# The chunk scan's factors and products kept in a PSUM bank instead of SBUF

## The chip, the cores and the metric

The kernel runs on one core of one Trainium2 chip. A core has five engines that run side by side, each with its own instruction queue in a fixed order: TensorE (PE in the profile, with its weight loads as PEld), VectorE (DVE), ScalarE (ACT), GpSimd (POOL) and SyncE (SP), which issues the DMA transfers. The metric is device time in microseconds, lower is better; a run's time is compared as the median of several executions.

## The reference, cut to what matters

Two layers of a trunk with parallel token mixers are run over 128 context tokens and 512 noisy tokens, width 1024. In each layer the modulated input goes through one wide projection, whose parts feed attention, a state-space branch, a Fourier branch and three gates. The branch that matters here is the state space:

```python
for di in range(2):                               # forward, backward
    bu = einsum(u, bb)                            # complex, per group of 16 channels
    h[t] = lb * h[t - 1] + bu[t]                  # complex, 32 groups x 64 states
    y = y + Re(c * h)
ssm_y = gelu(y)
ssm_y = ssm_y * sigmoid(ssm_y @ w_glu + b_glu)
merged = g_a * (attn @ w_a) + g_s * (ssm_y @ w_s) + g_f * (four @ w_f)
```

The six modulation vectors of a layer are `silu(c) @ w_ada[l] + b_ada[l]`, for two conditioning vectors.

## The kernel before

Activations are stored channels on partitions, tokens along the row, in two halves of 256 and 384 tokens. Every large product is made from operands split into a high and a low fp32r part, so it is three matmuls (lines 129 to 131). A weight tile arrives by DMA (`wraw`, three buffers), ScalarE rounds it to the high part (`wh`, line 111), and VectorE, or GpSimd for the units named in `PZ`, `PU`, `PB` and `PO`, subtracts to get the low part (`wl`, line 112). These splits stand between TensorE and its next weight tile.

**The scan.** The recurrence runs over chunks of 8 tokens: 64 chunks of the noisy tokens, 16 of the context tokens. `ssm_scan` first fills `V` (tile `Vst`, in SBUF) with the chunk inputs: TensorE's products `psv` lie in PSUM banks of the pool tag `ss`, which has two, and are copied out by ScalarE and VectorE (lines 648 to 651). Then come 64 steps on VectorE. A step reads the state row `V[:, s]`, multiplies it by the 8-step transition factors (line 658: 128 x 128 elements, real and imaginary state each against a pair of factors), and adds the two products to row `s + 1` (line 661: two additions). The first 16 steps carry both token groups: two multiplications of 128 x 128 and two additions of 128 x 128; the other 48 steps have one multiplication of 128 x 128 and two additions of 128 x 64. That is 80 multiplications and 128 additions in a layer. The factors are a slice of `L8`, a small SBUF table of both layers; the products lie in `sc`, an SBUF tile with two buffers.

`ssm_out` reads the states (`Hr`, lines 675 to 678), TensorE forms the outputs `psy` in the same two `ss` banks (lines 689 and 691), and VectorE and ScalarE apply the gelu (lines 694 to 698). Its result goes through DRAM to the product with `w_glu`.

**What runs beside it.** The scan is traced inside the stream of the wide projection (`mm_wz`): after its first four tiles the stream goes on with the gates, and the splits of their weights share VectorE's queue with the scan. In layer 0 two more things do. The modulation vectors that layer 0 still needs are made by VectorE as sums along rows of the transposed weights (`ada_rows`, line 276: a `scalar_tensor_tensor` of two SBUF tiles with its elementwise result in the PSUM tile `adjunk`), one step of four such sums each time the stream calls `fill`. And GpSimd makes the state-space tables of layer 1 (`ssm_prep`, lines 576 to 630: products of SBUF tiles, with transposes on TensorE between them), along with the low parts of some weight tiles. In layer 1 there are no such sums and no tables to make, so the same scan has only weight splits beside it.

**Order.** The order within each engine's queue is not written out by hand: the kernel is built with `schedule_with_timeline_sim=True`, by which the builder places instructions on a simulated timeline. A different instruction form can thus move its neighbours in the queues.

Of the kernel before, what the change touches and what calls it, by code (L numbers as in the profile page):

```python
# [10 lines left out]
F32 = mybir.dt.float32  # L11
# [6 lines left out]
DRAM = bass.MemoryType.DRAM  # L18

P = 128  # L20
# [41 lines left out]
class Trunk:  # L62
# [12 lines left out]

    # ---------------------------------------------------------------- helpers
    def mmbank(self, nm):
# [6 lines left out]
    def mmextra(self, n):  # L84
        """n more banks for the main products until the returned stack closes."""
        st = ExitStack()
        self.mmpool = st.enter_context(self.tc.tile_pool(name=f"mmx{self.mmi}", bufs=1, space=PSUM))
        self.mmx = n

        def off():  # L90
            self.mmx = 0
        st.callback(off)
        return st

    def behind(self, ins):
        """What is traced within on the engine of ins is queued behind it."""
        return nullcontext() if ins is None else self.tc.issue_after(ins.ins)

    def ld(self, dst, src):
        """A transfer; the first ones are issued as traced, and all others after them."""  # L100
        i = self.nc.sync.dma_start(dst, src)
        if self.head is not None:
            self.tc.add_manual_dep(i.ins, self.head.name, mybir.DependencyInfo(
                mybir.DependencyClass.NoSync, mybir.DependencyReason.DATA), reason="after the first loads")
        if self.pin:
            self.head = i.ins
        return i
# [25 lines left out]
    def wextra(self, pool, nm, n):  # L133
        """n more units for the weights of a stream."""
        return [[pool.tile([P, 1024], F32R, name=f"{nm}{k}{x}") for x in "hl"] for k in range(n)]

    def stream(self, tiles, operand, consume, lag, extra=(), fill_from=0, loaded=None, order=(1, 0), pool=(), pre=()):
        """tiles: list of (key, unit source, n, offsets); one half `lag` tiles behind the other;
        low parts of the units named in pool are taken by the Pool engine; pre: banks of tiles whose first half is there."""
        loaded = {} if loaded is None else loaded  # L140
        n = len(tiles)

        def go(j, half):
            key, src, width, offs = tiles[j]
            if half == order[0] and j in pre:
                return consume(key, half, pre[j][:, :HW[half]])
            if src not in loaded:
                k = len(loaded) % (4 + len(extra))
                loaded[src] = self.wunit(self.usrc(src), width, extra[k - 4] if k >= 4 else None,
                                         self.nc.gpsimd if len(loaded) in pool else None)  # L150
            h, l = loaded[src]
            pairs = []
            for kt, o in enumerate(offs):
                xh, xl = operand(half, kt, key)
                pairs.append((h[:, o:o + P], l[:, o:o + P], xh, xl))
            ps = self.mmbank(src[0])
            self.mm3(ps[:, :HW[half]], pairs)
            consume(key, half, ps[:, :HW[half]])

        for j in range(n + lag):  # L160
            if j < n:
                go(j, order[0])
            if j >= fill_from:
                self.fill()
            if j >= lag:
                go(j - lag, order[1])
# [8 lines left out]
    def rsqrt(self, out, v, tmp, iters=3):  # L175
        """out = v ** -0.5, v > 0; tmp: two scratch APs of the same shape."""
        nc = self.nc
        a, b = tmp
        nc.vector.tensor_scalar(a.bitcast(I32), v.bitcast(I32), 1, None, op0=OP.logical_shift_right)
        nc.vector.tensor_scalar(out.bitcast(I32), a.bitcast(I32), -1.0, float(0x5F3759DF), op0=OP.mult, op1=OP.add)  # L180
        nc.vector.tensor_scalar(a, v, -0.5, None, op0=OP.mult)
        for _ in range(iters):
            nc.vector.tensor_tensor(b, out, out, OP.mult)
            nc.vector.tensor_tensor(b, b, a, OP.mult)
            nc.vector.scalar_tensor_tensor(out, b, 1.5, out, OP.add, OP.mult)

    # ---------------------------------------------------------------- constants
    def constants(self):
# [6 lines left out]

    # ---------------------------------------------------------------- modulation
    def silu_c(self):
# [17 lines left out]
    def crows(self):  # L215
        """Silu of the conditioning vectors, as rows in DRAM scratch."""
        nc = self.nc
# [10 lines left out]
    def ada_first(self, pool, block):  # L228
        """Shift and scale of the first layer, by channel tiles."""
        nc = self.nc  # L230
# [29 lines left out]
    def ada_rows(self, l, vecs, cuts, part, bufs):  # L260
        """Modulation vectors of a layer as sums along rows of the transposed weights, in steps."""
        nc = self.nc
# [23 lines left out]
    def adpool(self, l):  # L286
        """Modulation vectors of a layer, in idle slots until closed."""
        st = ExitStack()
# [20 lines left out]
    def derive_u(self, l):  # L309
        """Per-channel scale and bias of u from x (first layer) or from the normalised rows."""  # L310
        nc, s, m = self.nc, self.small, self.mod[l]
# [27 lines left out]
    def modsplit(self, src, half, sc, sh, dt, uh, ul):  # L339
        """uh + ul = src * sc + sh on one channel tile of a half."""  # L340
        nc = self.nc
# [15 lines left out]

    # ---------------------------------------------------------------- layer norm
    def shift(self, r, out):
        """Take each token's mean over the channels off, which the layer norm ignores."""  # L360
        nc = self.nc
# [13 lines left out]
    def ln_add(self, st, half, r, dt):  # L375
        """Sums over the channel tiles of r and of its square."""
        nc = self.nc
# [15 lines left out]
    def ln_half(self, st, n, mm=False, later=None):  # L393
        """Banks with rstd and mean * rstd of each token, the same on every partition; mm: banks of the main products."""
        nc, m = self.nc, self.main
# [17 lines left out]
        out = []  # L413
# [6 lines left out]

    # ---------------------------------------------------------------- state-space tables
    def ssm_scalars(self, p, loads):
        """Powers of the discretised transition and of the input factor, both layers."""
        nc, tc = self.nc, self.tc
# [115 lines left out]
    def ssm_open(self):  # L540
        """Pools of the per-layer tables and the loads they start from."""
        st = self.prep = ExitStack()
# [16 lines left out]
    def ssm_prep(self, l, order):  # L559
        """Per-layer stationary operands of the chunked scan, left in DRAM scratch."""  # L560
        nc, tc = self.nc, self.tc
# [70 lines left out]

    # ---------------------------------------------------------------- state-space branch
    def ssm_scan(self, l, z, zp, V, U):
# [3 lines left out]
        for ch in range(8):  # L638
            w = z.tile([P, 4, 2, P], F32, name="wbs", tag="wbs", bufs=2)
            self.ld(w.rearrange("p g r q -> p (g r q)"), self.wbd[l][ch])  # L640
            for hh in range(2):
# [9 lines left out]
                nc.scalar.copy(V[bw, VP + 1:VP + 17, gr], v[bw, :16][:, ::-1])  # L651
        la = self.L8[:, :, 32 * l:32 * l + 32]
        for s in range(64):
            n = 2 if s < 16 else 1
            t = z.tile([P, 2, 2, 64], F32, name="sc", tag="sc", bufs=2)
            for k in range(n):
# [45 lines left out]

    # ---------------------------------------------------------------- one layer
    def layer(self, l):
# [204 lines left out]
    def ln_last(self, s, r, half, g, b, out):  # L909
        """The layer norm that ends the last layer."""  # L910
        nc = self.nc
# [38 lines left out]

    # ---------------------------------------------------------------- Fourier branch
    def fourier(self, fd, fh, fl):
# [53 lines left out]

    # ---------------------------------------------------------------- attention branch
    def qkv(self, l, z):
# [129 lines left out]
    def prompt_heads(self, z, zp, kv, QT, KTt, vt, ah, al):  # L1138
        """The context tokens' attention, four heads of one key head at a time."""
        nc = self.nc  # L1140
# [43 lines left out]

    # ---------------------------------------------------------------- gated MLP
    def ffn(self, l, u2, rh, resid, g2):
# [84 lines left out]

    # ---------------------------------------------------------------- program
    def run(self, layers=NL):
# [70 lines left out]
def _layout(a):  # L1344
    """Host side: slices, transposes, repeats and shape-only constants."""
    f = np.float32
# [101 lines left out]
```

## Time and profile before

| | |
|---|---|
| median of 3 executions | 2339.52 us (2337.55 to 2341.88) |
| profiled execution: span from first to last instruction | 2343.4 us |
| profiled execution: own time | no figure beside the span |
| PE busy | 2201.9 us (94%) |
| VectorE busy | 1699.0 us (73%) |
| ScalarE busy | 874.7 us (37%) |
| GpSimd busy | 627.3 us (27%) |

Busy is the time in which an engine had an instruction in work, so an instruction that has started and is held up counts as busy too. The span is 3.9 us above the median of the timed runs (0.17%). In the views "x" is a number of instructions; PEclk is the mean granted clock of TensorE as a share of its upper level, 2.4 GHz.

### The profile page before, as it was taken

How to read it: one execution, taken by the hardware profiler on the slowest of the kernel's cores; microseconds unless marked ns; L12 is line 12 of the kernel's file. 1: busy time of each engine (PE TensorE's matmuls, PEld its weight loads, DVE VectorE, ACT ScalarE, POOL GpSimd, SP SyncE). 2: the span in 40 equal slices, each digit the busy share in tenths (PEclk: the TensorE clock that was granted, in tenths of full speed). 3: DMA queues.
4: the chain of work that ended last, by engine and by line, in shares of the span. 5: the costliest groups of instructions: out<-in, count | busy, mean ns of one | idle time of the engine just before them, and what ended most of it. 6: DMA issues, size and time to landing. Idle time of an engine off the chain costs nothing.

```text
span 2343.4 us, 40415 instructions
## 1 busy us (share of the span) xinstructions
PE 2201.9 (94%) x15368; PEld 2122.0 (91%) x15368; DVE 1699.0 (73%) x3997; ACT 874.7 (37%) x1781; POOL 627.3 (27%) x603
## 2 busy tenths in 40 slices
PE   5998876998999999999998999999899999999997
PEld 4888776998879999999998999999879999999997
DVE  7779998779655888999986167455765876475476
ACT  4333212433643542332344332334463443243242
POOL 3337765003535410100116000001635420000003
PEclk8999897999999999999999999999999999999998
DMA  9976436664214124545535744742304122222221
GB/s 258 220 248 204 150 112 195 220 192 124 59 32 137 64 73 144 158 142 160 170 100 152 161 148 127 180 156 81 100 1 150 55 72 64 82 73 72 82 73 45
DMA packets 185009, 295.00 MB, mean 126 GB/s; under 512 B 48464, under 2 KB 127472, under 8 KB 184816
## 3 DMA queue, kind: packets, MB, share of 16 engines
q1 hardware_dynamic: 184816, 292.43, 42.4%
q8 instruction: 121, 1.98, 0.4%
q14 instruction: 72, 0.59, 0.1%
HBM read 242.62 MB, written 49.75 MB: 125 GB/s over the span
## 4 chain that ended last, share of the span: by engine, by line
PE 67%; DVE 16%; DMA 6%; issue 2%; ACT 1%; SPq 1%; POOL 1%; ACTq 0%; DVEq 0%; POOLq 0%
PE mm_w_up L130 7%; PE mm_w_up L131 7%; PE mm_w_up L129 7%; DVE adjunk L276 5%; PE mm_w_down L129 4%; PE mm_w_down L131 4%; PE mm_w_down L130 4%; PE mm_wz L130 3%; PE mm_wz L131 3%; PE mm_wz L129 3%; PE mm_pv L1129 2%; DMA araw<-in_w_ada_t_dram 2%; DVE Vst L661 2%; PE S L1171 2%; PE pt L1182 2%
## 5 line engine op out<-in xcount | busy, mean ns | idle before, releaser
L111 ACT CAST wh<-wraw 128x1024 fp32r<-128x1024 f32 (+1 forms) x226 | 234.6, 1038 | 430.5 <-PE mm_w_down L130 107.7
L129 PE MATMUL mm_w_up<-uh,wh 128*128 128x256 f32 (+1 forms) x1280 | 392.6, 309 | 2.6 <-DVE acc L1207 1.8
L130 PE MATMUL mm_w_up<-ul,wh 128*128 128x256 f32 (+1 forms) x1280 | 394.8, 309 | 0.0
L131 PE MATMUL mm_w_up<-uh,wl 128*128 128x256 f32 (+1 forms) x1280 | 394.3, 309 | 0.0
L112 POOL TENSOR_TENSOR wl<-wraw,wh 128x1024 fp32r<-128x1024 f32 x64 | 157.1, 2458 | 847.5 <-ACT wh L111 824.1
L276 DVE SCALAR_TENSOR_TENSOR adjunk<-araw,cb 128x512 f32<-128x512 f32 (+2 forms) x384 | 276.1, 719 | 45.7 <-DMA araw<-in_w_ada_t_dram 40.9
L131 PE MATMUL mm_wz<-uh,wl 128*128 128x384 f32 (+1 forms) x832 | 269.0, 324 | 23.2 <-DVE wl L112 23.2
L112 DVE TENSOR_TENSOR wl<-wraw,wh 128x1024 fp32r<-128x1024 f32 (+1 forms) x162 | 205.7, 1270 | 109.6 <-ACT wh L111 108.7
L129 PE MATMUL mm_wz<-uh,wh 128*128 128x384 f32 (+1 forms) x832 | 268.5, 324 | 5.2 <-ACT uh L111 3.5
L1207 DVE SCALAR_TENSOR_TENSOR acc<-mm_w_up,cw,acc 128x127 f32<-128x127 f32 (+2 forms) x616 | 229.3, 400 | 52.1 <-ACT acc L1213 32.9
L130 PE MATMUL mm_wz<-ul,wh 128*128 128x384 f32 (+1 forms) x832 | 267.0, 321 | 0.1
L129 PEld LDWEIGHTS mm_w_up<-uh,wh 128*128 128x128 f32 x1280 | 241.8, 189 | 3.2 <-issue 2.1
L130 PEld LDWEIGHTS mm_w_up<-ul,wh 128*128 128x128 f32 x1280 | 242.4, 189 | 0.5 <-DVE ul L112 0.5
L131 PEld LDWEIGHTS mm_w_up<-uh,wl 128*128 128x128 f32 x1280 | 242.3, 189 | 0.5 <-POOL wl L112 0.4
L131 PE MATMUL mm_w_down<-hh,wl 128*128 128x384 f32 (+1 forms) x656 | 203.0, 311 | 0.0
L130 PE MATMUL mm_w_down<-hh,wh 128*128 128x384 f32 (+1 forms) x656 | 202.8, 310 | 0.0
L129 PE MATMUL mm_w_down<-hh,wh 128*128 128x384 f32 (+1 forms) x656 | 200.7, 311 | 1.9 <-ACT wh L111 1.9
L131 PEld LDWEIGHTS mm_wz<-uh,wl 128*128 128x128 f32 x832 | 165.0, 198 | 25.3 <-DVE wl L112 24.4
L129 PEld LDWEIGHTS mm_wz<-uh,wh 128*128 128x128 f32 x832 | 165.7, 199 | 7.4 <-ACT uh L111 3.8
L130 PEld LDWEIGHTS mm_wz<-ul,wh 128*128 128x128 f32 x832 | 164.8, 198 | 2.3 <-issue 1.4
L129 PEld LDWEIGHTS mm_w_down<-hh,wh 128*128 128x128 f32 x656 | 123.4, 189 | 2.2 <-ACT wh L111 2.2
L1213 ACT ACTIVATE acc<-mm_w_up,cw 128x256 f32<-128x256 f32 (+1 forms) x176 | 107.2, 613 | 46.0 <-PE mm_w_up L131 44.5
(444 smaller groups left out, 5316.9 us busy)
## 6 DMA issues: line engine op xcount, KB each, us to landing
wraw<-in_w_up_dram SPq DMA_DIRECT2D x88, 512.0 KB, 3.6
wraw<-in_wz_dram SPq DMA_DIRECT2D x64, 512.0 KB, 3.9
araw<-in_w_ada_t_dram SPq DMA_DIRECT2D x48, 512.0 KB, 3.8
wraw<-in_w_down_dram SPq DMA_DIRECT2D x32, 512.0 KB, 3.6
araw<-in_w_ada_t_dram SPq DMA_DIRECT2D x32, 384.0 KB, 4.1
wraw<-in_w_br_dram SPq DMA_DIRECT2D x24, 512.0 KB, 3.7
td<-gt SPq DMA_DIRECT2D x48, 192.0 KB, 3.1
tl<-td SPq DMA_DIRECT2D x48, 192.0 KB, 3.1
```

The costliest lines, as they stand in the source:

```text
L111: nc.scalar.copy(h, src)
L112: return (eng or nc.vector).tensor_tensor(l, src, h.bitcast(F32), OP.subtract)
L129: mm(ps, wh, xh, start=j == 0, stop=False)
L130: mm(ps, wh, xl, start=False, stop=False)
L131: mm(ps, wl, xh, start=False, stop=j == n - 1)
L276: nc.vector.scalar_tensor_tensor(junk[:, :k.stop - k.start], raw[:, d], 1.0, cb[v], OP.mult, OP.mult, accum_out=part[:, c, vec - a, dt + d ...
L661: nc.vector.tensor_tensor(o, o, t[:, a, :n], OP.add)
L1129: nc.tensor.matmul(po[64 * hh:64 * hh + 64, :256], vt[:, kt + 1, kv * 64:kv * 64 + 64], PT[hh][:, kt], start=kt == 0, stop=kt == 5, tile_p ...
L1171: nc.tensor.matmul(S[:, b, :384], q, kt[:, hl, P + b * 384:P + (b + 1) * 384], start=hl == 0, stop=hl == 1)
L1182: nc.tensor.transpose(pt[:, j * P:(j + 1) * P], p[:, (3 * b + j) * P:(3 * b + j + 1) * P], self.ident)
L1207: nc.vector.scalar_tensor_tensor(o, src, w, o, OP.mult, OP.add)
L1213: nc.scalar.activation(acc, ps, AF.Identity, bias=b, scale=w1)
```

## The change

The factors of the layer and the products move from SBUF into one PSUM bank. The bank is a third user of the pool tag `ss`: columns 0 to 255 take the products, columns 256 to 383 the factors, which one ScalarE copy in each layer brings there from `L8`. The SBUF tile `sc` with its two buffers is gone, so consecutive steps write their products to the same place. Each multiplication now reads one operand from SBUF (`V`) and one from PSUM and writes to PSUM; each addition reads one operand from SBUF (`V`) and one from PSUM and writes to SBUF. The number, shapes and engine of the scan's instructions stay as they are, as do the modulation sums. The rest of the diff removes comments and docstrings.

```diff
@@ ssm_scan
-        la = self.L8[:, :, 32 * l:32 * l + 32]
+        bank = zp.tile([P, 512], F32, name="scb", tag="ss", bufs=2)
+        la = bank[:, 256:384].rearrange("p (a g r) -> p a g r", a=2, r=2)
+        nc.scalar.copy(la, self.L8[:, :, 32 * l:32 * l + 32])
+        t = bank[:, :256].rearrange("p (a k q) -> p a k q", a=2, k=2)
         for s in range(64):
             n = 2 if s < 16 else 1
-            t = z.tile([P, 2, 2, 64], F32, name="sc", tag="sc", bufs=2)
             for k in range(n):
                 h = V[:, s + VP * k].rearrange("p (g r) -> p r g", r=2).unsqueeze(3).broadcast_to((P, 2, 32, 2))
                 nc.vector.tensor_tensor(t[:, :, k].rearrange("p a (g r) -> p a g r", r=2), h, la, OP.mult)
```

## Rows read from the trace of the kernel before

**Rows 1.** Busy time of the whole page.
```profile
PE 2201.9 (94%) x15368; PEld 2122.0 (91%) x15368; DVE 1699.0 (73%) x3997; ACT 874.7 (37%) x1781; POOL 627.3 (27%) x603
```

**Rows 2.** Busy time by stretch: PE, PEld, DVE, ACT, POOL, PEclk, DMA share, GB/s.
```profile
80.00:207.00 127.00, 118.98 (x983) 114.27 (x982) 98.58 (x188) 48.20 (x121) 65.11 (x80) 0.96 0.87 244
207.00:365.00 158.00, 116.56 (x823) 111.45 (x821) 149.50 (x311) 33.11 (x67) 109.33 (x128) 0.85 0.43 141
207.00:440.00 233.00, 185.94 (x1307) 178.67 (x1306) 207.37 (x428) 55.60 (x112) 142.27 (x158) 0.85 0.53 165
440.00:600.00 160.00, 146.29 (x1017) 141.45 (x1016) 132.15 (x388) 60.70 (x128) 31.50 (x21) 0.98 0.52 160
1369.00:1457.00 88.00, 88.00 (x602) 88.00 (x601) 70.62 (x227) 23.66 (x40) 0.00 (x0) 1.00 0.40 125
```

**Rows 3.** Line 658 alone by stretch: DVE busy, PEclk, DMA share, GB/s.
```profile
207.00:440.00 233.00, 39.41 (x78) 0.85 0.53 165
1369.00:1457.00 88.00, 21.44 (x78) 1.00 0.40 125
```

**Rows 4.** Line 661 alone by the same stretches.
```profile
207.00:440.00 233.00, 61.49 (x128) 0.85 0.53 165
1369.00:1457.00 88.00, 30.92 (x128) 1.00 0.40 125
```

**Rows 5.** Groups of DVE from 368 to 425 us: count, busy us, mean ns, idle before.
```profile
L676 DVE COPY Hr<-Vst 64x512 f32<-64x512 f32 x6 | 5.6, 937 | 0.0
L696 DVE TENSOR_TENSOR ga<-ga,psy 128x320 f32<-128x320 f32 x8 | 3.9, 486 | 0.3
L698 DVE SCALAR_TENSOR_TENSOR Yh<-ga,psy 128x320 f32<-128x320 f32 x8 | 3.9, 483 | 2.8 <-DMA yd<-Yh 2.2 <-ACT ga L697 0.5
```

**Rows 6.** Line 1207 from 780 to 1230 us: durations in ns, min/median/max.
```profile
L1207 DVE SCALAR_TENSOR_TENSOR acc<-mm_w_up,cw,acc x308: 200/344/619, 788.1 to 1213.0; 128x127 f32<-128x127 f32 x87, 128x383 f32<-128x383 f32 x46, 128x1 f32<-128x1 f32 x21
L1207 DVE SCALAR_TENSOR_TENSOR acc<-edge,cw,acc x44: 201/209/1872, 808.9 to 1210.2; 128x1 f32<-128x1 f32 x44
```

**Rows 7.** Who PE waited for, 200 to 420 us: total, times, longest.
```profile
PE mm_wz L131 <- DVE wl L112: 23.2, 6, 7.6
PE psy L691 <- DVE Hr L678: 18.9, 1, 18.9
PE psy L689 <- DVE Yh L698: 4.0, 2, 2.5
```

**Rows 8.** Shares by line of the chain that ended last, 200 to 400 us.
```profile
by line: DVE Vst L661 25.5%; DVE adjunk L276 24.4%; DVE sc L658 17.3%; DMA araw<-in_w_ada_t_dram 10.6%; issue 5.3%; DVE wl L112 5.0%; DMA wcs<-wcd 3.6%; PE psy L691 1.3%; DVE Hr L678 1.3%; DVE ga L695 1.1%; DVE Hr L677 0.9%; PE pkp L626 0.9
```

**Rows 9.** Line 658 from 1366 to 1460 us, groups as in rows 5.
```profile
L658 DVE TENSOR_TENSOR sc<-Vst,L 128x128 f32<-128x128 f32 x78 | 21.4, 291 | 2.1
```

**Rows 10.** Groups of DVE over the whole span, each shape apart.
```profile
L1237 DVE TENSOR_TENSOR th<-th,acc 128x384 f32<-128x384 f32 x44 | 24.1, 549 | 0.0
L830 DVE SCALAR_TENSOR_TENSOR tl<-tl,mm_w_br 128x384 f32<-128x384 f32 x32 | 17.6, 550 | 23.6 <-PE mm_w_br L131 21.5 <-POOL mt L831 1.9 <-issue 0.2
L112 DVE TENSOR_TENSOR al<-mm_pv,ah 128x128 fp32r<-128x128 f32 x16 | 4.5, 284 | 10.5 <-ACT ah L111 10.2
L866 DVE SCALAR_TENSOR_TENSOR mt<-mm_w_out,g,mt 128x128 f32<-128x128 f32 x32 | 9.6, 342 | 4.2 <-PE mm_w_out L131 4.2
```

**Rows 11.** Line 276 from 205 to 370 us, groups as in rows 5.
```profile
L276 DVE SCALAR_TENSOR_TENSOR adjunk<-araw,cb 128x384 f32<-128x384 f32 x50 | 45.3, 905 | 4.8 <-DMA araw<-in_w_ada_t_dram 4.8
```

**Rows 12.** A group of ACT, 200 to 212 us.
```profile
L648 ACT COPY Vst<-psv 64x256 f32<-64x256 f32 x2 | 0.7, 367 | 2.4 <-PE psv L644 2.4
```

**Rows 13.** Who POOL waited for, 207 to 440 us: total, times, longest.
```profile
POOL wl L112 <- ACT wh L111: 21.2, 5, 10.0
POOL wct L600 <- DMA wcd<-wct: 17.1, 4, 5.9
```

**Rows 14.** Who PE waited for, 1300 to 1560 us.
```profile
PE psy L691 <- DMA wcs<-wcd: 1.1, 1, 1.1
```

**Rows 15.** Who DVE waited for, 207 to 440 us.
```profile
DVE adjunk L276 <- DMA araw<-in_w_ada_t_dram: 16.2, 8, 4.0
```

## The prediction, made before the change was run

> **What bounds the kernel now.** I read the page first: TensorE is busy 94% of the span and VectorE 73% [rows 1]. A kernel like that gains from a faster VectorE only where TensorE waits for it, so I went on to the stages. The busy times by stretch show one stage that stands out [rows 2]. From 207 to 440 us, which is layer 0 from the start of the scan to the end of the wide projection, TensorE is busy 185.94 of 233 us, so it is idle for 47.1; VectorE is busy 207.37 of 233, and in the scan's own part, 207 to 365 us, 149.50 of 158. TensorE's mean granted clock there is 0.85, between its two levels of 1.2 and 2.4 GHz, against 0.96 in the stretch before and 1.00 around layer 1's scan. The list of waits says what TensorE's idle time is: 23.2 us for low parts of weights that VectorE had not yet made, 18.9 us in one piece for the states that the scan leaves, 4.0 us for the gelu's results [rows 7]. All three are VectorE being late. The chain that ended last agrees: between 200 and 400 us the scan's two lines are 25.5% + 17.3% = 42.8% of it, 86 us, and the modulation sums 24.4% [rows 8].
>
> Why is VectorE late there? The scan runs twice with the same instructions, so the two layers can be set side by side. The multiplications take 39.41 us in layer 0 and 21.44 in layer 1, for 78 recorded instructions each [rows 3]; the additions 61.49 and 30.92, for 128 each [rows 4]. The scan is therefore stretched in layer 0 by 17.97 + 30.57 = 48.5 us. What differs is GpSimd: 142.27 us busy in the one stage, 0.00 in the other [rows 2].
>
> Which instructions are stretched is the point on which the change turns. In layer 0's gelu, with GpSimd still at work (142.27 - 109.33 = 32.9 us between 365 and 440 [rows 2]), the two instructions that take one operand from PSUM keep to 486 and 483 ns, while a copy of 512 elements out of SBUF takes 937 ns [rows 5]. The MLP gives the cleanest comparison: the same line at widths down to one element, and GpSimd takes part of the weight splits meanwhile. The 308 additions that read a PSUM operand never pass 619 ns, which is what the widest of them takes; the 44 of one element that take all from SBUF have a median of 209 and a maximum of 1872 [rows 6]. So an instruction that reads PSUM and SBUF isn't held up by GpSimd, and one with all its inputs in SBUF is. The change moves the scan from the second kind into the first.
>
> **The change, part by part.**
>
> *The relief.* Nothing is removed in number: 80 multiplications and 128 additions in each layer. If all run in layer 0 as they do in layer 1, VectorE has 48.5 us less to do between 207 and 365 us. In layer 1 there is nothing to relieve, since GpSimd is idle, and TensorE is busy for all of those 88 us anyway [rows 2].
>
> *The price of PSUM operands.* The trace has no multiplication that reads and writes PSUM, so I bound it. Below: a subtraction of 128x128 with one PSUM operand takes 284 ns [rows 10], the scan's multiplication of the same size, all in SBUF, 291 [rows 9]; at 384 elements 550 with PSUM and 549 without [rows 10]. Writing to PSUM is what the modulation sums' elementwise result does already. That makes the price nothing. Above: the residual's 128x128 with PSUM takes 342 ns [rows 10], though it also takes a per-partition factor; against 291 that is 51 ns, times 208 instructions 10.6 us for a layer. I take nothing, since the instructions nearest in kind (two tensors, no per-partition factor) say so, and keep 10.6 us for the range. The Trainium skill speaks against the change here: "VectorE: DVE Perf Modes", in its section on the TRN2 errata, gives VectorE a fixed part of 58 cycles from SBUF and 120 from PSUM. By its 0.96 GHz that is an estimate of 65 ns for an instruction and 13.4 us for the 208 of layer 0, and the forecast below would be later by as much; the rows just read (284 against 291, 550 against 549) don't show such a step.
>
> *The factors' copy.* One ScalarE copy of 128x128 in each layer, between the copy of 64x256 that takes 367 ns [rows 12] and nothing. It needs the bank of the last but one `psv`, which is emptied before the scan can start; behind it on ScalarE's queue wait the roundings of weights and, with them, TensorE. Twice 0.4 us at most, taken as nothing.
>
> *The bank.* It holds one of the two `ss` banks until the scan's last addition. The first `psy` can still start early in the other; the second can't. But each `psy` ends in a product with the states, so nothing is completed later. One product buffer in place of two costs nothing, as a step's multiplication waits for the additions before it in any case.
>
> *What takes over.* The modulation sums still read two SBUF tiles: 905 ns in the scan's stage [rows 11] against about 549 for that width where nothing interferes [rows 10], 50 x 0.356 = 17.8 us of stretch that stays. With fewer scan instructions in GpSimd's way, GpSimd's own work packs closer, and sums and splits may meet it more often; its waits for layer 1's tables to be stored (17.1 us) and for rounded weights (21.2 us) [rows 13] then come sooner too. VectorE's waits for weight rows (16.2 us [rows 15]) come from the transfers and stay.
>
> *The sum.* Two ceilings for the stage of 233 us: VectorE, 207.4 - 48.5 = 158.9 busy plus its present idle time of 25.6 gives 184.5, a gain of 48.5. TensorE, 185.9 busy at the present clock and no idle, a gain of 47.1; at the clock of the stretch before (0.96) it would need less. It won't reach no idle time: in that stretch, 80 to 207 us, with GpSimd also at work, it is idle 8.0 of 127 us, 6.3% [rows 2]. 185.9 / 0.937 = 198.4 us, a gain of 34.6, call it 35. The rest of the layer follows in the same order and starts earlier; TensorE is then busy 146.29 of 160 us [rows 2], so little is lost behind. The profiled execution gives 2343.4 - 35 = 2308.4 us; its span stands 3.9 us over the median of the runs, so the forecast is 2339.5 - 35 = **2304.5 us**.
>
> **The rivals.**
>
> *The stage finds another holder.* VectorE gets its time back, but TensorE then waits for roundings, for GpSimd's splits or for transfers. If of TensorE's three waits only the one in a single piece goes, the gain is 18.9: 2320.6 us. For it: GpSimd's queue holds weight splits among the tables, and the tables' transfers (17.1 us of its waits) don't get faster. Against it: its longest wait is for rounded weights, 21.2 us [rows 13], and a rounding needs one of the four `wh` buffers, which TensorE gives back late as long as it waits for VectorE.
>
> *PSUM operands have their price.* With the upper bound, 10.6 us for layer 0's scan, the gain is 35 - 10.6 = 24.4: 2315.1 us. For it stands only the row with a per-partition factor, against it the other two pairs [rows 9, 10]. It would end the gain altogether only at 48.5 / 208 = 233 ns for an instruction. This is the rule of "VectorE: DVE Perf Modes" in the Trainium skill as this kernel would feel it.
>
> *The relief isn't there.* What GpSimd's work holds up could be any access of VectorE to SBUF; the additions still read and write `V` there. Then the time stays 2339.5. Against it stand the 308 additions and the gelu, which read and write SBUF beside a PSUM operand and aren't stretched [rows 5, 6].
>
> *Slower: the new order of the queues.* The builder places instructions by simulated times, and these may differ for PSUM operands. If VectorE's splits fall behind more steps of the scan, or TensorE's products with the states are placed further ahead of the scan's end, TensorE waits longer in layer 0. Its three waits on VectorE sum to 46.1 us [rows 7]; a second helping of them gives 2304.5 + 46.1 = 2350.6. It decides when the new waits pass the 35 us of relief. Nothing in the trace of before can show it; in layer 1, where the order is as free, TensorE waits only 1.1 us for any of this [rows 14].
>
> **How the numbers follow.** The forecast's case, a gain of 25 to 48.5 us, gets 0.63; the other holder, 5 to 25 us, 0.15; the price of PSUM operands, 0.06, about as much gain; no relief 0.08; slower 0.08. A measurement of this kernel tells 0.2%, 4.7 us, from no change. So faster 0.84, same 0.08, slower 0.08. The range runs from the ceiling, 2339.5 - 48.5 = 2291, rounded to 2290, to 2330, which takes in most of the second case and all of the third; the forecast's own is 2291 to 2315.
>
> **What the profile would show.** Line 658 near 291 ns and line 661 near layer 1's durations in both layers; layer 0's sum over both lines near 52 us in place of 101. TensorE's wait for the states short or gone, its waits for low parts of weights less than half, and its clock between 207 and 400 us nearer 0.96. Line 276 still stretched, at 0.9 us or more. Layer 1's scan stage unchanged. The prediction is wrong in its mechanism if line 661 still has maxima over 1 us, in its price if layer 1's scan gets longer per instruction, and in its carry if VectorE is relieved by 48 us and the end of layer 0's wide projection moves by under 25.

## The result, and the profile after

The changed kernel took 2315.33 us (median of 4 runs, 2312.68 to 2319.53) beside 2339.18 us for the kernel before on the same chip: a ratio of 0.9899, interval 0.9885 to 0.9913. It is 24 us faster where 35 was forecast, inside the range of 2290 to 2330 and 0.3 us outside the forecast's own range of 2291 to 2315. The profiled execution of the changed kernel took 2312.68 us with a span of 2310.9. The two spans differ by 32.5 us, more than the medians do: in the profiled execution of before, layer 1's wide projection took 277 us and here 271, and in the other profiles it varies between 268 and 278 us without following the change. Below, layer 0 is read from the traces and the end from the medians.

All line numbers from the scan on are two higher: the multiplication is line 660, the addition 663, the factors' copy 654. First the busy time of the page (compare [rows 1]):

```profile
PE 2186.2 (95%) x15368; PEld 2107.1 (91%) x15368; DVE 1662.5 (72%) x3997; ACT 875.6 (38%) x1783; POOL 632.2 (27%) x603
```

VectorE has 36.5 us less to do. The durations of the scan's instructions in both layers, in ns (minimum, median, maximum), with the first and the last start:

```profile
L663 DVE TENSOR_TENSOR Vst<-Vst,scb x256: 206/220/289, 212.3 to 1434.4; 128x64 f32<-128x64 f32 x96, 128x128 f32<-128x128 f32 x32
L660 DVE TENSOR_TENSOR scb<-Vst,scb x160: 281/295/330, 209.3 to 1431.3; 128x128 f32<-128x128 f32 x160
L654 ACT COPY scb<-L x2: 269/278/286, 202.9 to 1342.5; 128x128 f32<-128x128 f32 x2
```

The same view of the kernel before, which [rows 3, 4] give only by stretch:

```profile
L661 DVE TENSOR_TENSOR Vst<-Vst,sc x256: 215/226/2262, 207.7 to 1455.4; 128x64 f32<-128x64 f32 x96, 128x128 f32<-128x128 f32 x32
L658 DVE TENSOR_TENSOR sc<-Vst,L x160: 277/292/1390, 82.9 to 1452.3; 128x128 f32<-128x128 f32 x160
```

Maxima of 2262 and 1390 ns are gone: not one of the 416 instructions passes 330 ns, in layer 0 as in layer 1. By stretch, line 660 alone and then line 663 alone (busy time, count, PEclk, DMA share, GB/s), to be read against [rows 3, 4]:

```profile
207.00:440.00 233.00, 24.10 (x80) 0.90 0.59 182
1342.00:1435.00 93.00, 23.61 (x80) 1.00 0.40 126
...
207.00:440.00 233.00, 30.00 (x128) 0.90 0.59 182
1342.00:1435.00 93.00, 30.32 (x128) 1.00 0.40 126
```

Layer 0's scan is down from 39.41 + 61.49 = 100.9 us to 24.10 + 30.00 = 54.1, a relief of 46.8 us. Layer 1's was 21.44 + 30.92 = 52.4 and is 53.9. The windows of the kernel before hold 78 of each layer's 80 multiplications because two ran ahead of them, in layer 0 at 82.9 and 91.1 us; in the changed kernel all 80 lie inside. That is 0.6 us of each comparison.

The same stretches for all engines (PE, PEld, DVE, ACT, POOL, PEclk, DMA share, GB/s; compare [rows 2]). The wide projection of layer 0 ended at 446.4 us (the prediction had put its end at 440) and now ends at 425.9:

```profile
80.00:207.00 127.00, 117.32 (x995) 112.16 (x993) 95.98 (x186) 49.30 (x124) 65.96 (x83) 0.99 0.86 248
207.00:365.00 158.00, 129.44 (x938) 124.28 (x938) 135.52 (x348) 36.89 (x73) 130.91 (x140) 0.90 0.53 164
207.00:440.00 233.00, 198.32 (x1419) 190.88 (x1418) 191.51 (x478) 62.41 (x122) 147.92 (x155) 0.90 0.59 182
207.00:426.00 219.00, 186.06 (x1337) 178.82 (x1337) 178.21 (x443) 57.10 (x112) 147.92 (x155) 0.89 0.59 181
1342.00:1435.00 93.00, 93.00 (x640) 93.00 (x639) 72.50 (x230) 25.20 (x46) 0.00 (x0) 1.00 0.40 126
```

From 207 us to the end of the stage TensorE is idle 219 - 186.06 = 32.9 us, 15%; in the kernel before it was idle 47.1 of the 239.4 us to that end. Its busy time in the stage fell too, from 192.3 to 186.1 us, at a granted clock of 0.89 in place of 0.86. What it waits for, 200 to 420 us (total, times, longest; compare [rows 7]):

```profile
PE psy L693 <- DVE Hr L680: 17.1, 1, 17.1
PE mm_wz L131 <- DVE wl L112: 10.5, 6, 2.9
PE psy L691 <- DVE Yh L700: 2.6, 1, 2.6
```

The splits are sooner done, but the single piece for the states is still there. So I went to what VectorE does between the scan's steps: the groups of 205 to 370 us (count, busy us, mean ns, idle before; compare [rows 11]), then who it waited for from 207 to 440 us [rows 15]:

```profile
L276 DVE SCALAR_TENSOR_TENSOR adjunk<-araw,cb 128x384 f32<-128x384 f32 x56 | 61.4, 1097 | 16.7 <-DMA araw<-in_w_ada_t_dram 16.6
L112 DVE TENSOR_TENSOR wl<-wraw,wh 128x1024 fp32r<-128x1024 f32 x8 | 13.0, 1630 | 0.0
```
```profile
DVE adjunk L276 <- DMA araw<-in_w_ada_t_dram: 22.9, 13, 4.0
```

A modulation sum, not touched by the change, has gone from 905 to 1097 ns, and VectorE waits 16.7 us for weight rows in that window where it waited 4.8. GpSimd, for its part, got more done beside the scan: it is busy 130.91 us between 207 and 365, in place of 109.33. The sums and the scan's steps stand in order on the same queue. For an account of the scan alone, the window has to end with the scan's last addition, which starts at 353.3 us in place of 369.2. For the kernel before, the sums of that window are those of [rows 11]; for the changed kernel, from 205 to 353.6 us, they are

```profile
L276 DVE SCALAR_TENSOR_TENSOR adjunk<-araw,cb 128x384 f32<-128x384 f32 x54 | 60.3, 1116 | 16.6 <-DMA araw<-in_w_ada_t_dram 16.6
```

The lines of the scan give back 46.8 us. The sums take 60.3 - 45.3 = 15.0 of it, the waits ahead of them 16.6 - 4.8 = 11.8, the splits 13.0 - 10.6 = 2.4, and the first copies of the states (`Hr`) 10.6 - 6.4 = 4.2. That leaves 13.4 us, where the last addition comes 15.9 earlier: neighbouring instructions overlap a little, so the account closes only to within some 3 us. The product with `w_glu` starts at 425.7 in place of 446.3 (20.6 earlier), that with `w_out` at 675.8 in place of 697.9 (22.1), and the end comes 24 earlier. In the chain that ended last, 200 to 400 us, the sums and their rows have gone from 35.0% to 42.3%, and the scan's two lines from 42.8% to 9.6% (compare [rows 8]):

```profile
by line: DVE adjunk L276 23.0%; DMA araw<-in_w_ada_t_dram 19.3%; PE psy L693 6.6%; DVE wl L112 6.2%; issue 5.8%; DVE Vst L663 5.2%; DVE scb L660 4.4%; PE psy L691 3.2%; DMA td<-gt 2.8%; DMA wraw<-in_wz_dram 2.7%; DMA wcs<-wcd 2.6%; DVE Hr L
```

### The profile page after: what moved, and what is told of

The parts are those of the page before. It is cut to its first block, busy times and chain, and to the rows that moved or that the text cites. A ratio compares the mean times of both kernels' runs of the same rounds, so it can differ in the third digit from the quotient of the medians.

```text
span 2310.9 us, 40415 instructions
## 1 busy us (share of the span) xinstructions
PE 2186.2 (95%) x15368; PEld 2107.1 (91%) x15368; DVE 1662.5 (72%) x3997; ACT 875.6 (38%) x1783; POOL 632.2 (27%) x603
## 4 chain that ended last, share of the span: by engine, by line
PE 67%; DVE 18%; DMA 9%; issue 3%; ACT 2%; SPq 1%; POOL 1%; ACTq 0%; DVEq 0%
PE mm_w_up L130 7%; PE mm_w_up L131 7%; PE mm_w_up L129 7%; DVE adjunk L276 6%; DMA araw<-in_w_ada_t_dram 4%; PE mm_wz L130 4%; PE mm_wz L129 4%; PE mm_wz L131 4%; PE mm_w_down L131 4%; PE mm_w_down L129 4%; PE mm_w_down L130 4%; PE mm_pv L1131 2%; PE mm_w_br L129 2%; PE mm_w_br L130 2%; PE mm_w_br L131 2%
## 5 line engine op out<-in xcount | busy, mean ns | idle before, releaser
L276 DVE SCALAR_TENSOR_TENSOR adjunk<-araw,cb 128x512 f32<-128x512 f32 (+2 forms) x384 | 284.1, 740 | 53.1 <-DMA araw<-in_w_ada_t_dram 48.2
L131 PE MATMUL mm_wz<-uh,wl 128*128 128x384 f32 (+1 forms) x832 | 263.3, 317 | 11.0 <-DVE wl L112 10.5
L129 PE MATMUL mm_wz<-uh,wh 128*128 128x384 f32 (+1 forms) x832 | 262.8, 317 | 5.6 <-ACT uh L111 3.9
L1209 DVE SCALAR_TENSOR_TENSOR acc<-mm_w_up,cw,acc 128x127 f32<-128x127 f32 (+2 forms) x616 | 229.2, 400 | 52.1 <-ACT acc L1215 32.9
L131 PEld LDWEIGHTS mm_wz<-uh,wl 128*128 128x128 f32 x832 | 159.9, 192 | 13.7 <-DVE wl L112 11.9
L129 PEld LDWEIGHTS mm_wz<-uh,wh 128*128 128x128 f32 x832 | 160.5, 193 | 7.3 <-ACT uh L111 4.2
L130 PEld LDWEIGHTS mm_wz<-ul,wh 128*128 128x128 f32 x832 | 160.1, 192 | 2.5 <-issue 1.8
L131 PEld LDWEIGHTS mm_w_down<-hh,wl 128*128 128x128 f32 x656 | 123.2, 188 | 1.0 <-DVE wl L112 0.9
```

The costliest lines, as they stand in the source:

```text
L129: mm(ps, wh, xh, start=j == 0, stop=False)
L130: mm(ps, wh, xl, start=False, stop=False)
L131: mm(ps, wl, xh, start=False, stop=j == n - 1)
L276: nc.vector.scalar_tensor_tensor(junk[:, :k.stop - k.start], raw[:, d], 1.0, cb[v], OP.mult, OP.mult, accum_out=part[:, c, vec - a, dt + d ...
L1209: nc.vector.scalar_tensor_tensor(o, src, w, o, OP.mult, OP.add)
```

## The experiments

My theory: GpSimd holds up the VectorE instructions that have all inputs in SBUF, and what one group no longer suffers the next such group does (the hand-on), the sums above all, which then also run ahead of their weight rows. The rivals: that half of the change (factors or products) does it all; that the bank, the copy or the price of PSUM operands takes part of the gain back; that the new order of the queues does. All ratios are to the kernel before on the same chip; e6, e8, e11 and e12 ran on other chips than the runs that they are set against, and the ratios give the same differences as the medians within 1.5 us.

### One half, then the other

```diff
 e1: products back in SBUF
-        t = bank[:, :256].rearrange("p (a k q) -> p a k q", a=2, k=2)
+            t = z.tile([P, 2, 2, 64], F32, name="sc", tag="sc", bufs=2)
 e2: factors back in SBUF
-        la = bank[:, 256:384].rearrange("p (a g r) -> p a g r", a=2, r=2)
-        nc.scalar.copy(la, self.L8[:, :, 32 * l:32 * l + 32])
+        la = self.L8[:, :, 32 * l:32 * l + 32]
```

> Theory A (an instruction of VectorE whose inputs all lie in SBUF is held up by GpSimd's work, one with a PSUM input is not; only the multiplications are relieved here): in layer 0 the multiplications are near 291 ns on average and near 24 us in sum, the additions keep their 61 us or get worse, up to 70, as GpSimd packs closer. Time: the multiplications' part of the stretch, 18 of 48.5 us, of the change's gain of 24, so about 9 us under the kernel before, 2330 us (2324 to 2337). Theory B (the gain comes from the new order of the queues or from giving up the product buffers, and the stretch has another cause): both lines stretched, and a time that has nothing to do with the share, 2339 or 2315 us.

> Theory A: the additions are relieved, near 31 us in layer 0, the multiplications keep 39 us or get worse, up to 50. Time: 30.6 of 48.5 us of the stretch, so about 15 us under the kernel before, 2324 us (2318 to 2332). Theory B: both lines alike, and 2339 or 2315 us.

Factors alone: 2334.11 us, ratio 0.9981 (0.997 to 0.9992). Products alone: 2338.54 us, ratio 1.0001 (0.9988 to 1.0015). VectorE's groups of 205 to 370 us, first of e1, then of e2:

```profile
L276 DVE SCALAR_TENSOR_TENSOR adjunk<-araw,cb 128x384 f32<-128x384 f32 x53 | 55.5, 1048 | 8.8 <-DMA araw<-in_w_ada_t_dram 8.6
L663 DVE TENSOR_TENSOR Vst<-Vst,sc 128x64 f32<-128x64 f32 x96 | 42.6, 444 | 2.5
L660 DVE TENSOR_TENSOR sc<-Vst,scb 128x128 f32<-128x128 f32 x80 | 21.4, 284 | 1.7
L663 DVE TENSOR_TENSOR Vst<-Vst,sc 128x128 f32<-128x128 f32 x32 | 19.7, 616 | 0.7
```
```profile
L276 DVE SCALAR_TENSOR_TENSOR adjunk<-araw,cb 128x384 f32<-128x384 f32 x55 | 56.6, 1030 | 7.2 <-DMA araw<-in_w_ada_t_dram 7.1
L659 DVE TENSOR_TENSOR scb<-Vst,L 128x128 f32<-128x128 f32 x80 | 55.2, 690 | 2.0
L662 DVE TENSOR_TENSOR Vst<-Vst,scb 128x64 f32<-128x64 f32 x96 | 20.9, 218 | 2.6
L662 DVE TENSOR_TENSOR Vst<-Vst,scb 128x128 f32<-128x128 f32 x32 | 9.1, 284 | 0.8
```

Each half does to its own line what the whole does (284 ns; 218 and 284 ns), and each loses much of it elsewhere: with the additions relieved by 31.5 us, the multiplications, whose instruction is that of before but for where its result goes, take 55.2 us in place of 39.4, past the 50 that I had allowed. In time, e1 came out as expected; e2, expected at 2318 to 2332, did not. A small account shows the hand-on. Against layer 1's times before (multiplications 22.0 us for 80, additions 30.9) and 549 ns for an undisturbed sum of 384 columns [rows 3, 4, 10], the stretch that GpSimd causes in this window is

```
us         sums   multiplications   additions   together   without a hand-on
before     17.9        18.0            30.6        66.4
e1         26.4        -0.6            31.4        57.2        48.4
e2         26.4        33.2            -0.9        58.7        35.8
changed    30.7         2.1            -0.9        31.9        17.8
```

for 50, 53, 55 and 56 sums. The last column is the row of before less the stretch of the relieved lines. A half frees 18 or 31 us and keeps 9 or 8 of it. The halves gain 4.6 and 0.2 us of time, the whole 24: they aren't additive, and no half does it all.

### Without layer 1's tables

e3 is the kernel before, e4 the changed one, both without `ssm_prep` of layer 1, GpSimd's main work beside the scan (layer 1 then reads layer 0's tables). e11 is e3 with the bank taken and the factors copied there, which only the scan's last step reads.

```diff
-                self.ssm_prep(l + 1, (1,))
+                self.wbd[1], self.wcd[1], self.pd[1] = self.wbd[0], self.wcd[0], self.pd[0]
```

> Leaves out the tables of layer 1 (layer 1 reads layer 0's), so GpSimd has little to do beside layer 0's scan; the scan itself is as in the kernel before. Theory A: multiplications and additions in layer 0 take what they take in layer 1, about 21 and 31 us, with everything in SBUF, and the modulation sums fall to about 0.6 us each. The time falls by more than the change's gain, since the tables' own matmuls go too: about 2295 us (2275 to 2312). Theory B: the scan's lines stay stretched in layer 0 (39 and 61 us).

> The changed kernel without the tables of layer 1. Theory A: with GpSimd idle there is nothing to relieve, so this run is within 5 us of the same cut in the kernel before. Theory B: the change is worth its 24 us here as well.

> Layer 1's tables left out, scan in SBUF, but the bank is taken and the factors are copied into it, and the last step reads them there, so the bank is held as long as in the changed kernel. With the tables left out the changed scan took 2301 us and the scan before 2292. Theory E (the bank, which one psy tile has to wait for, and the copy cost those 9 us): 2298 to 2304 us. Theory F (they come from the order of the queues, which the builder makes from other simulated durations for PSUM operands): 2290 to 2295 us, and TensorE doesn't wait for the states as it does there (13.5 us).

e3: 2292.46 us, ratio 0.9811 (0.9794 to 0.9828). e4: 2301.16 us, ratio 0.9839 (0.9817 to 0.986). e11: 2293.54 us, ratio 0.9814 (0.9798 to 0.9829). With everything in SBUF and the tables gone, the scan's stretch is all but gone; e3, same columns:

```profile
L276 DVE SCALAR_TENSOR_TENSOR adjunk<-araw,cb 128x384 f32<-128x384 f32 x73 | 52.2, 715 | 31.9 <-DMA araw<-in_w_ada_t_dram 31.6
L661 DVE TENSOR_TENSOR Vst<-Vst,sc 128x64 f32<-128x64 f32 x96 | 23.5, 245 | 2.4
L658 DVE TENSOR_TENSOR sc<-Vst,L 128x128 f32<-128x128 f32 x78 | 23.5, 317 | 1.5
```

That is GpSimd as the cause, by taking its tables away; but with the tables go their transposes on TensorE, their copies on ScalarE and their transfers. The traces separate these. Take the scan's two lines and the sums that start between 200 and 445 us, and call an instruction stretched when it takes over 1.15 times the shortest of its shape. In the kernel before, 93 of 289 are stretched, and each of the 93 overlaps a GpSimd instruction; of the 145 that overlap none, not one is. In e3, where GpSimd has only eight splits of weights and one more instruction left in that time, 9 of 330 are stretched, again each beside one of these, and none of the 319 clear of them. These few are what still lifts the sums of e3 to a mean of 715 ns. One pair of e3 (start in us, duration in us):

```profile
270.21 2.60 POOL L112 TENSOR_TENSOR wl<-wraw,wh 128x1024 fp32r<-128x1024 f32 x1 [5.84 <-ACT wh L111]
270.48 2.48 DVE L658 TENSOR_TENSOR sc<-Vst,L 128x128 f32<-128x128 f32 x1
```

The multiplication, 291 ns where nothing interferes, ends 0.15 us after the split. So it is throughout: in the kernel before, all 93 end shortly after a GpSimd `tensor_tensor` has ended: 78 to 84 ns for 64 columns, 144 to 151 for 128, 420 to 426 for 384. They are held until that instruction is over.

e3 also shows the other half of the story: relieved of GpSimd, the sums run into their weight rows, 31.6 us in this window.

e4 was expected to match e3 within 5 us and is 8.7 slower by the medians, though the ranges of their 4 runs meet (2294.93 to 2305.56 against 2291.74 to 2297.52). If it is real, it is a cost of the change where it relieves nothing. The bank and the copy aren't it: e11 has both and stands 1.1 us from e3. Nor are durations: 305 ns against 317 for the multiplication, 219 against 245 for the addition. The difference is there in full when `w_glu` starts (406.6 against 397.9 us). What differs is the order on VectorE's queue: 93 sums start ahead of the scan's last addition in e4 and 88 in e3 and e11, and from 200 to 430 us VectorE waits 43.8 us for weight rows against 34.4 and 41.1. e11 is fast with nearly the same wait, so that isn't proof. What the 8.7 us are stays open.

### The sums in PSUM too

If the sums inherit the stretch, giving them a PSUM operand should end it. In e5 ScalarE copies layer 0's two vectors into the PSUM bank where the elementwise result was, which goes to SBUF; a bank holds them in pieces of 256 columns, so there are 64 loads of 256 columns in place of 32 of 384 and 16 of 256. e7 is the changed kernel with those cuts alone, e6 the kernel before with e5's sums.

```diff
-        junk = self.adp.tile([P, 512], F32, name="adjunk")
+            junk = self.adj.tile([P, 256], F32, name="adjunk")
+            cps = self.adp.tile([P, 2, 256], F32, name="cbp")
...
+                for v in range(2):
+                    nc.scalar.copy(cps[:, v], cb[v])
+                cb = [cps[:, v] for v in range(2)]
...
-            vecs, cuts = V0, (0, 384, 768, 1024)
+            vecs, cuts = V0, (0, 256, 512, 768, 1024)
```

> On the changed kernel, layer 0's modulation sums read their vectors from a PSUM bank too (ScalarE copies them there, 256 columns of each vector at a time; the elementwise result goes to SBUF, and there are 64 weight loads of 256 columns instead of 48 of 384). Theory A (what the scan no longer suffers, the sums took over, 0.9 to 1.1 us each, and that is why 24 and not 35 us arrived): the sums take about 0.43 us each, VectorE has another 25 us or more free in the stage, and the time falls by 5 to 12 us under the changed kernel, to 2303 to 2310 us. Theory C (the sums' transfers hold the queue: VectorE waits in order for weight rows, 26 us in the changed kernel against 10 before): the sums get shorter, their waits for transfers longer by as much, and the time stays at 2315 within 4 us or rises with the larger number of loads.

> Control for the run before: the changed kernel with 64 loads of 256 columns, and the sums' vectors in SBUF as they were. VectorE has 64 more sums with their fixed parts, by the profile's 0.43 + 0.14 us against 0.55 + 0.14 about 14 us more work in all. Theory A: more collisions, so slower than the changed kernel, 2318 to 2328 us. Theory C: two things against each other, smaller transfers but more of them; 2312 to 2322 us.

> The scan as in the kernel before (all in SBUF), layer 0's sums with their vectors in PSUM and 64 loads of 256 columns. Theory D (collisions are handed on: GpSimd's instructions meet whichever of VectorE's still have all inputs in SBUF, so relieving one group alone lengthens the other): the sums take about 0.42 us, and the scan's two lines in layer 0 stay at their 101 us or go above it; the time is 15 to 35 us over the run that has both in PSUM (2312), 2327 to 2347 us. Theory A alone (each group's relief stands for itself): the scan's lines unchanged at 101 us, and the time 24 us over it, 2336 us. The two are told apart by the scan's sum, not by the time.

e5: 2311.97 us, ratio 0.9895 (0.9871 to 0.9919), no better than the change, where theory A had 2303 to 2310; nor did the waits for rows grow, as theory C had it (24.9 us from 200 to 430 us, 26.1 in the changed kernel). e7: 2343.18 us, ratio 1.0028 (1.0004 to 1.0053): the smaller cuts alone cost more than the whole gain, 28 us against the changed kernel, where I had expected 13 at most. e6: 2345.95 us, ratio 1.004 (1.0025 to 1.0056). In e5 no sum of layer 0 is held up; durations in ns as above:

```profile
L284 DVE SCALAR_TENSOR_TENSOR adjunk<-araw,cbp x256: 406/420/431, 127.0 to 545.0; 128x256 f32<-128x256 f32 x128
```

Under e7's same cuts the sum of 256 columns takes 723 ns (205 to 440 us), so the PSUM vectors are worth 31 us of time, e7 against e5. Not all of that is relief from GpSimd: the read of each sum's accumulator, an instruction of its own, takes 83 ns in the median in e5 and 140 in e7, some 15 us less VectorE time for 256 sums. In e6 the sums are as quick (416 ns) and the hand-on runs the other way, into the scan; e6, 205 to 440 us:

```profile
L670 DVE TENSOR_TENSOR Vst<-Vst,sc 128x64 f32<-128x64 f32 x96 | 49.2, 513 | 2.6
L667 DVE TENSOR_TENSOR sc<-Vst,L 128x128 f32<-128x128 f32 x78 | 40.0, 528 | 1.6
L284 DVE SCALAR_TENSOR_TENSOR adjunk<-araw,cbp 128x256 f32<-128x256 f32 x92 | 38.3, 416 | 14.2 <-DMA araw<-in_w_ada_t_dram 13.1
L670 DVE TENSOR_TENSOR Vst<-Vst,sc 128x128 f32<-128x128 f32 x30 | 18.8, 626 | 0.7
```

513 ns where the kernel before has 453 for the first group, and 108 us for the scan's lines in place of 100.9. With the sums out of GpSimd's way the change is worth 34.0 us (e6 against e5), near the 35 that I had forecast for it alone; as e5 and e6 also have other cuts and loads, the closeness is in part luck.

Why e5 has no more than the change, although its scan ends at 314.0 us and `w_glu` starts at 396.4, 29 earlier: as I read it, the sums lag behind. 180 of the 256 come after the scan's last addition, and they end at 545 us. They share their row buffers with the stream's weights, and from 380 to 460 us the DMA queue waits 21.7 us for sums to give buffers back; own buffers, below, test this. TensorE's two longest waits from 200 to 700 us in e5, of which the changed kernel lacks the first and has 2.9 us of the second:

```profile
PE mm_w_br L129 <- ACT wh L111: 15.8, 1, 15.8
PE ptq L1113 <- DVE qs L1110: 13.8, 6, 4.9
```

### Own buffers for the weight rows

e9 gives e5's loads two buffers of 2 KB a partition of their own, e12 one (`bufs=1`); e8 gives them to e7, with the sums' vectors in SBUF.

```diff
-                    raw = self.wp.tile([P, 2, 512], F32, name="araw", tag=ART, bufs=AB)[:, :, :k.stop - k.start]
+                    raw = (self.wp.tile([P, 2, 512], F32, name="araw", tag=ART, bufs=AB) if l else self.adj.tile([P, 2, 256], F32, name="araw", tag="araw", bufs=2))[:, :, :k.stop - k.start]
```

> As the run with the sums' vectors in PSUM, and layer 0's weight rows for the sums get two buffers of their own instead of sharing three with the stream's weights, so that a load can start before a weight tile is given back. Theory A: the same as without the own buffers within 4 us. Theory C: VectorE's waits for weight rows fall to under half, and the time falls by 8 to 20 us under the changed kernel, 2295 to 2307 us.

> The changed kernel once more, for a second profile: which of its differences from before stand in both executions. 2312 to 2319 us; multiplications and additions near 24 and 30 us in layer 0; TensorE's wait for the states again near 17 us.

> The changed kernel with 64 loads of 256 columns and two buffers of their own for layer 0's weight rows; the sums' vectors stay in SBUF. Against the run with shared buffers (2343) the own buffers alone should give what they gave beside PSUM vectors, 16 us: 2327 us (2318 to 2335). Against the run with both (2296) it shows what the sums' PSUM vectors are worth once the transfers no longer hold them: by theory A and D 20 to 35 us, with sums at 0.65 us or more here.

> As the best version so far (scan and sums with PSUM operands, own buffers for the sums' weight rows), but with one own buffer instead of two. With two, the builder puts 158 sums between the scan's first and last addition, with one 77, so the scan should end 81 sums of 0.55 us, some 40 us, of VectorE work earlier less the longer waits for rows, at 310 to 325 instead of 344 us, and TensorE's waits for the scan's results (6.1 and 17.6 us) should go. If the sums left for later don't hold the attention's start as they did with the shared buffers, the time falls to 2280 to 2290 us; if they do, as in the run with shared buffers (30 us of TensorE's waits between 500 and 560 us), 2296 to 2312 us. Which of the two weighs more can't be told from the rows; I take 2292.

e9: **2296.4 us** (2294.39 to 2297.82), ratio 0.9824 (0.9807 to 0.9842). The changed kernel again, on that chip: 2314.63 us, ratio 0.9902 (0.9887 to 0.9917), with 24.1 and 30.0 us for layer 0's multiplications and additions, 1088 ns for a sum and a wait of 17.1 us for the states, as in its first profile. So e9 beats both kernels, this one by 18 us. The time is as expected, the way there is not: VectorE's waits for rows, which were to fall to under half, are 25.2 us from 207 to 440 us, against 24.5 in e5. What the own buffers changed is the order: 222 of the 256 sums start ahead of the scan's last addition, against 76 in e5. They run from 69.6 to 392.7 us, so none is left to hold up the attention; TensorE's longest waits (200 to 700 us) are now for the gelu's result on its way through DRAM and 6.1 us, no longer 17, for the states. VectorE's waits for rows, then TensorE's:

```profile
DVE adjunk L284 <- DMA araw<-in_w_ada_t_dram: 25.2, 24, 4.1
```
```profile
PE mm_w_glu L129 <- DMA yb<-yd: 17.6, 1, 17.6
PE psy L702 <- DVE Hr L689: 6.1, 1, 6.1
```

e8: 2349.7 us, ratio 1.0053 (1.0035 to 1.0071), far from the 2327 expected and no better than e7, whose interval it meets. With buffers of their own the sums move ahead of the scan (221 ahead of its last addition, 76 in e7) while each still suffers; 205 to 440 us of e8, and TensorE's longest waits:

```profile
L276 DVE SCALAR_TENSOR_TENSOR adjunk<-araw,cb 128x256 f32<-128x256 f32 x184 | 147.7, 803 | 8.8 <-DMA araw<-in_w_ada_t_dram 6.5 <-DMA cb<-cd 1.5
```
```profile
PE psy L694 <- DVE Hr L681: 19.8, 1, 19.8
PE ptp L614 <- POOL wbt L603: 18.6, 3, 9.5
PE mm_wz L131 <- DVE wl L112: 15.6, 5, 5.1
```

The scan then ends at 397.7 us. The waits for rows are short (6.5 us, 26.6 in e7, 207 to 440 us) and the kernel is no faster: taking those waits away gained nothing by itself. Between e8 and e9 only the place of the vectors, with their copies, and of the elementwise result differs, 53 us.

e12: 2311.63 us, ratio 0.9894 (0.9861 to 0.9926), expected at 2292, or 2296 to 2312 if the sums left for later held up the attention. Its scan ends at 326.1 us and `w_glu` starts at 398.1, earlier than in e9 (344.3 and 408.1), but as in e5 sums are left over, 40 us of them from 390 to 560, and hold up the attention, so that `w_out` starts at 670.2 against 650.1:

```profile
PE S L1182 <- DVE adjunk L284: 13.0, 1, 13.0
```

## Why the prediction was right, and where its size was off

**The mechanism: right.** An instruction with one input in PSUM isn't held up by GpSimd: maxima of 330 and 289 ns where they were 1390 and 2262, with GpSimd busy for 147.92 us beside it; 170 of layer 0's 208 overlap a GpSimd instruction. e3 and the overlaps show from the other side that GpSimd was the cause.

**The relief: right.** 48.5 us forecast, 46.8 measured on the two lines; their sum 54.1, forecast near 52.

**The price of PSUM operands: right, as near nothing as can be told.** The median multiplication takes 295 ns in place of 292 and the addition 220 in place of 226; layer 1's scan took 0.9 us more for the same number. The rule of the Trainium skill in "VectorE: DVE Perf Modes" (section on the TRN2 errata) weighed there would, by the estimate made from it, have added 65 ns to each of these; the measured rows don't show it for fp32 tensor by tensor operations, and they decide.

**The copy and the bank: right.** 278 ns each, and e11, with both and no use of them but one, is 1.1 us from e3.

**The sums: wrong in size.** I let their stretch stay at 17.8 us, with a warning that they might meet GpSimd more often; it became 30.7. The waits for weight rows, "come from the transfers and stay", grew from 16.2 to 22.9 us. Both stood on VectorE's queue ahead of the scan's later steps. That GpSimd's work would pack closer and meet the sums more often was foreseen and put at nothing in the sum; it did (130.91 us of GpSimd in place of 109.33 between 207 and 365).

**The sum: this is the term that was mis-sized.** I took VectorE's 48.5 us as given back in full and let TensorE's idle share fall to 6.3%, that of the stretch before. It fell to 15% (32.9 of 219 us): a gain of 20.6 us at the start of `w_glu`, not 34.6. Of that gain only 14.2 us is idle time, 20 short of the forecast; 6.3 came from TensorE's shorter busy time at the higher clock, which the sum had put at nothing. That the miss is no larger is luck to this extent. By the prediction's own test (VectorE relieved by 48 us, the stage's end moved by under 25) this step failed. The relief of one line had to be netted against the others that stand in GpSimd's way; e6 against e5 gives the 34 us only once the sums are out of it.

**The carry to the end: right.** 20.6 us at `w_glu`, 22.1 at `w_out`, 24 at the end; layer 1's scan stage still has TensorE busy throughout.

**The marks.** The waits for low parts of weights are under half (10.5 from 23.2), line 276 is above 0.9 us (1.097). The wait for the states, forecast short or gone, is 17.1 from 18.9: the wait ends 16.9 us earlier (348.7 in place of 365.7 us), but TensorE, with fewer waits for splits ahead, comes there 15.1 us earlier too. The clock rose from 0.85 to 0.90, half of the way to 0.96.

**The rivals.** A gain of 24 us lies in the band of the second case, another holder (5 to 25 us), but not by its mechanism: it expected the wait for the states to go and roundings, GpSimd's splits or transfers to hold TensorE. GpSimd's splits cost it 0.5 us, and the holder is VectorE still. No relief is refuted by the durations. The slower order of the queues didn't decide; e4 against e3 may show 8.7 us of it, which no run here separates from noise.

## What to carry to other kernels

When several groups of instructions share a resource that another engine holds up, cost the relief of one group net of what the others will take over, and expect halves of a change to be worth less than half; relieving all of them together paid here only once the sums' rows had buffers of their own as well (e9; e5, without these, has no more than the change). On a queue kept in order, ask of each neighbour what it waits for when it comes sooner, since what is queued behind it waits too. And a stall can disappear without the kernel getting faster (e8), so try the fix on the chip before counting its microseconds.

## What the runs showed of the hardware that I had not expected

The hold-up moves on in large part: with 31.5 us taken off the additions, the multiplications beside them, with their inputs untouched, took 15.8 us more, and the sums 125 ns more each (e2). A held-up instruction ended a nearly fixed time after the GpSimd `tensor_tensor` that it met, 78 to 84 ns for 64 columns and 420 to 426 for 384 in the kernel before. A sum of 256 columns took 415 to 420 ns with one input in PSUM and the elementwise result in SBUF, and 723 to 803 with both inputs in SBUF and the result in PSUM. What counted was where the inputs lay, not the result: e1's multiplications (one input in PSUM, result in SBUF) kept to 289 ns, e2's (inputs in SBUF, result in PSUM) went up to 2422. A single SBUF instruction could be held for over 2 us (2262 ns for an addition of 128x64 that takes 215 to 228 where no GpSimd instruction overlaps it).
